# A row softmax in 64 tiles: sixteen narrow loads at the start, and a new order of the last two tiles

## The chip, the cores and the metric

The kernel runs on one core of a Trainium2 chip. The time is device time in microseconds (us) of one execution, and the median of several executions is what is compared. Besides the times there is a profile of one execution: it lists every instruction of each engine with its start and length, and every packet that the core's 16 DMA engines moved. The compute engines that matter here are VectorE (called DVE in the profile) and ScalarE (ACT). SyncE (SP) computes nothing; it issues the DMA transfers.

## The reference

The input is `logits`, 16 x 256 x 32,768 numbers in fp32, and a temperature, which is 1.0. The output is the softmax over the last axis:

```python
scaled = logits / temperature
scaled = scaled - scaled.max(axis=-1, keepdims=True)
exp_scaled = np.exp(scaled)
return (exp_scaled / exp_scaled.sum(axis=-1, keepdims=True)).astype(np.float32)
```

There are 4096 rows of 32,768 numbers, 512 MB in (536.87 million bytes) and as much out. Every number is read once and written once.

## The kernel before, in words

**Tiling.** Each row is cut into two halves of 16,384 numbers, which gives 8192 half rows; neighbours belong to one row. 128 half rows, one for each partition, make a tile of 8 MB. There are 64 tiles, numbered 0 to 63, and three buffers for them (`_BUFS`); tile g lives in buffer g mod 3, and everything is done in place: loaded, exponentiated, scaled and stored from the same memory.

**Work on a tile** (`compute`, lines 120 to 202). The tile is handled in K = 4 pieces of 4096 columns.
- For each piece VectorE takes the negated maximum of every partition (line 133) and ScalarE then computes exp(x - maximum of the piece) in place, with the sum of the piece beside it (line 146). Before its first maximum VectorE waits for the load.
- Then come the totals of the tile, a chain of small steps that passes between the engines: VectorE swaps the maxima and sums of neighbouring partitions, so that both halves of a row know all eight pieces (line 157), and takes the maximum over the eight (line 161); ScalarE computes the eight correction factors (line 168); VectorE sums factor times piece sum (line 174) and takes the reciprocal (line 186).
- At last VectorE multiplies every piece by its factor and by the reciprocal (line 193, "scaling" below).

**Order of the work.** It is written out by hand. Each engine runs its own instructions in program order and waits on semaphores. All transfers, loads and stores, are issued by SyncE into one queue, in the order of the list that `transfers` returns:

- L0 L1 L2, then S0 in two halves, L3 in two halves, S1, S2,
- then L4 S3, L5 S4, and so on up to L61 S60,
- then L62, L63, S61, S62, and S63 in four quarters.

A load of tile g (line 214) is issued once the store of tile g - 3 has landed, since they share a buffer. A store (line 223) is issued once all scaled pieces that it covers are done. Because the issuing engine goes through the list in order, a transfer that isn't ready holds up all that stand behind it. The transfers in the queue are carried out by 16 DMA engines at the same time, each of which takes a share of every transfer's rows in the queue's order.

**Where the change acts.** At the beginning L0 is one transfer of 128 rows x 16,384 columns, and `compute(0)` waits for all of it before its first maximum. At the end the engines' order is: everything of tile 62 (maxima, exponentials, totals, four scalings), then everything of tile 63. S62 needs four scaled pieces of tile 62; each quarter of S63 needs one scaled piece of tile 63.

Of the kernel before, what the change touches and what calls it, by code (L numbers as in the profile page):

```python
# [8 lines left out]
_W = 16384  # L9
_BUFS = 3  # L10
_PIECE = 4096
_LAST_STORE = 4096


class Stream:


    def __init__(self, nc, engine, name):
        self.engine = engine
        self.sem = nc.alloc_semaphore(name)  # L20
        self.count = 0
        self.seen = {}
# [38 lines left out]
def transfers(n):  # L61
    half = _W // 2  # L62
    whole = [(0, _W)]  # L63
    halves = [(0, half), (half, half)]
    quarters = [(s, _LAST_STORE) for s in range(0, _W, _LAST_STORE)]
    plan = [("L", 0, whole), ("L", 1, whole), ("L", 2, whole)]
    plan += [("S", 0, halves), ("L", 3, halves), ("S", 1, whole), ("S", 2, whole)]
    for i in range(4, n - 2):
        plan += [("L", i, whole), ("S", i - 1, whole)]
    plan += [("L", n - 2, whole), ("L", n - 1, whole)]  # L70
    plan += [("S", n - 3, whole), ("S", n - 2, whole), ("S", n - 1, quarters)]
    return plan


@with_exitstack
def kernel(
    ctx: ExitStack,
    tc: tile.TileContext,
    logits: bass.AP,
    temperature: bass.AP,  # L80
    out: bass.AP,
):
    nc = tc.nc
    inv_t = 1.0 / float(temperature)
    P = nc.NUM_PARTITIONS
    fp32 = mybir.dt.float32
    Exp = mybir.ActivationFunctionType.Exp
    A = mybir.AluOpType

    xf = logits.flatten_outer_dims()  # L90
    of = out.flatten_outer_dims()
    N, V = xf.shape
    assert V == 2 * _W and (N * 2) % P == 0
    x = xf.rearrange("n (h v) -> (n h) v", h=2)
    o = of.rearrange("n (h v) -> (n h) v", h=2)
    G = N * 2 // P
    K = _W // _PIECE
    swap = [i ^ 1 for i in range(32)]

    ctx.enter_context(tc.tile_critical())  # L100
    X = nc.alloc_sbuf_tensor("xs", [P, _BUFS * _W], fp32)
    T = [nc.alloc_sbuf_tensor(f"t{q}", [P, 4 * K], fp32) for q in range(2)]
    E = [nc.alloc_sbuf_tensor(f"ee{q}", [P, 2 * K], fp32) for q in range(2)]
    J = [nc.alloc_sbuf_tensor(f"junk{q}", [P, 2 * K], fp32) for q in range(2)]
    R = [nc.alloc_sbuf_tensor(f"row{q}", [P, 4], fp32) for q in range(2)]

    sp = Stream(nc, nc.sync, "sp")
    dve = Stream(nc, nc.vector, "dve")
    act = Stream(nc, nc.scalar, "act")
    loads = Lanes(nc, "ld")  # L110
    stores = Lanes(nc, "st")
    landed = {}
    stored = {}
    scaled = {}
    hist = {}

    def overlapping(parts, s, n):
        return [token for (a, m), token in parts.items() if a < s + n and s < a + m]

    def compute(g):  # L120
        base = (g % _BUFS) * _W
        t, e, j_, r = T[g % 2], E[g % 2], J[g % 2], R[g % 2]
        tv = t[:, 0 : 4 * K].rearrange("p (a b k) -> p a b k", a=2, b=2)
        old = hist.get(g - 2)
        if old:
            dve.wait(*old)
        sums = None
        for k in range(K):
            s = k * _PIECE
            xs = X[:, base + s : base + s + _PIECE]  # L130
            dve.wait(*overlapping(landed[g], s, _PIECE))
            m = dve.done(
                nc.vector.tensor_reduce(  # L133
                    out=t[:, k : k + 1], in_=xs, axis=mybir.AxisListType.X, op=A.max, negate=True
                )
            )
            if inv_t != 1.0:
                dve.wait(m)
                m = dve.done(
                    nc.vector.tensor_scalar_mul(  # L140
                        out=t[:, k : k + 1], in0=t[:, k : k + 1], scalar1=inv_t
                    )
                )
            act.wait(m)
            sums = act.done(
                nc.scalar.activation(  # L146
                    out=xs,
                    in_=xs,
                    func=Exp,
                    bias=t[:, k : k + 1],  # L150
                    scale=inv_t,
                    accum_out=t[:, K + k : K + k + 1],
                )
            )
        dve.wait(sums)
        sh = dve.done(
            nc.vector.stream_shuffle(out=t[:, 2 * K : 4 * K], in_=t[:, 0 : 2 * K], mask=swap)  # L157
        )
        dve.wait(sh)
        mx = dve.done(  # L160
            nc.vector.tensor_reduce(  # L161
                out=r[:, 0:1], in_=tv[:, :, 0, :], axis=mybir.AxisListType.XY, op=A.min
            )
        )
        act.wait(mx)
        ev = e[:, 0 : 2 * K].rearrange("p (a k) -> p a k", a=2)
        ee = act.done(
            nc.scalar.activation(  # L168
                out=ev, in_=tv[:, :, 0, :], func=Exp, bias=r[:, 0:1], scale=-1.0
            )  # L170
        )
        dve.wait(ee)
        tr = dve.done(
            nc.vector.tensor_tensor_reduce(  # L174
                out=j_[:, 0 : 2 * K].rearrange("p (a k) -> p a k", a=2),
                in0=ev,
                in1=tv[:, :, 1, :],
                scale=1.0,
                scalar=0.0,
                op0=A.mult,  # L180
                op1=A.add,
                accum_out=r[:, 1:2],
            )
        )
        dve.wait(tr)
        rc = dve.done(nc.vector.reciprocal(out=r[:, 2:3], in_=r[:, 1:2]))  # L186
        dve.wait(rc)
        scaled[g] = {}
        for k in range(K):
            s = k * _PIECE  # L190
            xs = X[:, base + s : base + s + _PIECE]
            scaled[g][s, _PIECE] = dve.done(
                nc.vector.tensor_scalar(  # L193
                    out=xs,
                    in0=xs,
                    scalar1=e[:, k : k + 1],
                    scalar2=r[:, 2:3],
                    op0=A.mult,
                    op1=A.mult,
                )  # L200
            )
        hist[g] = (ee, tr)

    for what, g, parts in transfers(G):
        base = (g % _BUFS) * _W
        rows = slice(g * P, (g + 1) * P)
        if what == "L":
            landed[g] = {}
            for k, (s, n) in enumerate(parts):
                if g >= _BUFS:  # L210
                    sp.wait(*overlapping(stored[g - _BUFS], s, n))
                landed[g][s, n] = loads.add(
                    (g % _BUFS, k),
                    nc.sync.dma_start(out=X[:, base + s : base + s + n], in_=x[rows, s : s + n]),
                )
            compute(g)
        else:
            stored[g] = {}
            for k, (s, n) in enumerate(parts):
                sp.wait(*overlapping(scaled[g], s, n))  # L220
                stored[g][s, n] = stores.add(
                    (g % _BUFS, k),
                    nc.sync.dma_start(out=o[rows, s : s + n], in_=X[:, base + s : base + s + n]),  # L223
                )
    sp.wait(*stores.tokens())
# [35 lines left out]
```

## Time and profile before

| what | value |
|---|---|
| median of 3 executions | 2514.72 us (2513.66 to 2514.77) |
| the profiled execution: its own time | 2513.76 us |
| its span, first to last instruction | 2512.0 us |
| moved by DMA | 1073.86 MB, 427 GB/s over the span |
| VectorE busy | 1755.7 us (70%) |
| ScalarE busy | 993.5 us (40%) |
| one maximum of a piece (line 133) | 4.41 us |
| one exponential of a piece (line 146) | 3.71 us |
| one scaling of a piece (line 193) | 2.41 us |

The profile's page gives busy times, the DMA traffic and groups of equal instructions. The other views are cut from the same execution: the *timeline* (instructions in order of time, with what ended the idle time before each), *windows* (busy time of each engine, share of time that the 16 DMA engines were busy, and GB/s, for a stretch of time), and the *DMA view* (packets of a stretch, and for the transfers issued in it the time from issue to landing; where there are several, the median). A DMA packet is counted in the stretch in which it starts, so a share over a short stretch can be above 1. A DMA transfer has landed when the last of its shares is through. A line such as `DVE t L133` means VectorE's work of line 133 that writes `t`. One core computes alone, and no other core's traffic is in the records.

### The profile page before, as it was taken

The numbers are of one execution on the slowest core, as the hardware profiler recorded it, in microseconds if no ns is written. First come the engines' busy times: TensorE is split into PE (matmuls) and PEld (weight loads), VectorE is DVE, ScalarE is ACT, GpSimd is POOL, SyncE is SP. The second block draws the span as 40 slices with busy tenths as digits, with TensorE's granted clock in tenths as the row PEclk, the third lists the DMA queues.
The fourth block names the chain that finished last, engine by engine and source line by source line (L and its number), as shares of the span: only waits on it lengthen the run. The fifth ranks groups of instructions, "written<-read, shape, count | busy, mean of one in ns | idle before, by whom it ended". The sixth has DMA issues, their size and how long they took to land.

```text
span 2512.0 us, 1661 instructions
## 1 busy us (share of the span) xinstructions
DVE 1755.7 (70%) x896; ACT 993.5 (40%) x577; POOL 0.2 (0%) x4
## 2 busy tenths in 40 slices
DVE  5866676766767667677676766777767676676776
ACT  3443342433424334243342433424334244342443
POOL 0000000000000000000000000000000000000000
DMA  9999999999999999999999999999999999999999
GB/s 409 443 427 432 434 432 432 425 432 432 420 433 425 429 431 422 432 424 430 433 421 431 434 427 425 434 431 422 433 432 421 431 422 433 433 420 432 434 420 389
DMA packets 19165, 1073.86 MB, mean 427 GB/s; under 512 B 2128, under 2 KB 2128, under 8 KB 2128
## 3 DMA queue, kind: packets, MB, share of 16 engines
q1 hardware_dynamic: 19152, 1073.75, 99.8%
q14 instruction: 13, 0.11, 0.0%
HBM read 536.87 MB, written 536.87 MB: 427 GB/s over the span
## 4 chain that ended last, share of the span: by engine, by line
DMA 57%; DVE 36%; ACT 5%; SPq 0%; issue 0%
DMA xs<-in_logits_dram 56%; DVE t L133 23%; DVE xs L193 12%; ACT xs L146 5%; DMA out_dram<-xs 1%; ACT ee L168 0%; SPq L223 0%; DVE row L186 0%; DVE row L161 0%; DVE t L157 0%; DVE junk L174 0%; DVE row L174 0%; SPq L256 0%; SPq L100 0%
## 5 line engine op out<-in xcount | busy, mean ns | idle before, releaser
L146 ACT ACTIVATE xs<-xs,t 128x4096 f32<-128x4096 f32 x256 | 949.2, 3708 | 1464.4 <-DVE t L133 1464.4
L133 DVE TENSOR_REDUCE t<-xs 128x1 f32<-128x4096 f32 x256 | 1113.4, 4412 | 462.1 <-DMA xs<-in_logits_dram 462.1
L193 DVE TENSOR_SCALAR xs<-xs,ee,row 128x4096 f32<-128x4096 f32 x256 | 600.4, 2409 | 2.3
L157 DVE LOAD_MASK_SELECT t<-t x64 | 0.9, 14 | 248.1 <-ACT xs L146 248.1
L146 ACT ACTIVATION_READ_ACCUMULATOR xs<-xs,t 128x1 f32 x256 | 47.7, 186 | 0.0
L168 ACT ACTIVATE ee<-t,row 128x8 f32<-128x8 f32 x64 | 19.2, 301 | 27.6 <-DVE row L161 27.6
L174 DVE CUSTOM_DVE_ANT_1 junk<-ee,t 128x8 f32<-128x8 f32 x64 | 10.7, 167 | 23.6 <-ACT ee L168 23.6
L186 DVE RECIPROCAL row<-row 128x1 f32<-128x1 f32 x64 | 10.5, 164 | 2.2
L161 DVE TENSOR_REDUCE row<-t 128x1 f32<-128x8 f32 x64 | 10.3, 161 | 2.2
L157 DVE STREAM_SHUFFLE t<-t 128x8 f32<-128x8 f32 x64 | 10.2, 160 | 0.0
L174 DVE DVE_READ_ACCUMULATOR2_ANT row<- 128x1 f32 x64 | 5.3, 83 | 0.0
L146 ACT ACT_TABLE_LOAD x1 | 1.3, 1283 | 0.9 <-SPq L100 0.9
L242 POOL MEMSET const-bfloat16-1.0<- 128x1 bf16 x1 | 0.1, 101 | 0.0
L242 POOL MEMSET const-uint8-127<- 128x1 uint8 x1 | 0.1, 101 | 0.0
L242 POOL MEMSET const-float32-0.0<- 128x1 f32 x1 | 0.1, 98 | 0.2 <-issue 0.2
L242 POOL MEMSET const-float32-1.0<- 128x1 f32 x1 | 0.1, 98 | 0.0
## 6 DMA issues: line engine op xcount, KB each, us to landing
out_dram<-xs SPq DMA_DIRECT2D x2, 4096.0 KB, 25.1
xs<-in_logits_dram SPq DMA_DIRECT2D x2, 4096.0 KB, 19.3
out_dram<-xs SPq DMA_DIRECT2D x4, 2048.0 KB, 10.8
xs<-in_logits_dram SPq DMA_DIRECT2D x63, 46.1
out_dram<-xs SPq DMA_DIRECT2D x62, 26.7
```

What stands on the lines that cost most here:

```text
L133: nc.vector.tensor_reduce(out=t[:, k : k + 1], in_=xs, axis=mybir.AxisListType.X, op=A.max, negate=True)
L146: nc.scalar.activation(out=xs, in_=xs, func=Exp, bias=t[:, k : k + 1], scale=inv_t, accum_out=t[:, K + k : K + k + 1],)
L157: nc.vector.stream_shuffle(out=t[:, 2 * K : 4 * K], in_=t[:, 0 : 2 * K], mask=swap)
L161: nc.vector.tensor_reduce(out=r[:, 0:1], in_=tv[:, :, 0, :], axis=mybir.AxisListType.XY, op=A.min)
L168: nc.scalar.activation(out=ev, in_=tv[:, :, 0, :], func=Exp, bias=r[:, 0:1], scale=-1.0)
L174: nc.vector.tensor_tensor_reduce(out=j_[:, 0 : 2 * K].rearrange("p (a k) -> p a k", a=2), in0=ev, in1=tv[:, :, 1, :], scale=1.0, scalar=0. ...
L186: rc = dve.done(nc.vector.reciprocal(out=r[:, 2:3], in_=r[:, 1:2]))
L193: nc.vector.tensor_scalar(out=xs, in0=xs, scalar1=e[:, k : k + 1], scalar2=r[:, 2:3], op0=A.mult, op1=A.mult,)
L242: nc = _bacc.Bacc("TRN2", target_bir_lowering=False, num_devices=1)
```

## The change

**At the start.** L0 covers the first 14,336 columns only. The last 2048 columns of tile 0 become an item of their own in the list ("N"), issued right behind: 16 transfers of 8 partitions each, in every group of 32 partitions the partitions j, j + 4, ..., j + 28 for j = 0 to 3. All 16 count on one semaphore. Tile 0's compute is written behind them; its pieces 0 to 2 now wait for the wide part alone, and piece 3 (columns 12,288 to 16,383) for both.

**At the end.** `compute` becomes a class `Tile` whose methods do what the sections of the old function did, in the same way: `exponentials` (maxima and exponentials of the pieces named), `totals`, and `scale`. Tiles 0 to 61 run them in the old order. For the last two tiles the order is

- exponentials of tile 62, all four pieces,
- exponentials of tile 63, the first piece,
- totals of tile 62,
- scaling of tile 62's pieces 0 and 1 on VectorE, and of its pieces 2 and 3 on ScalarE (`scale_on_act`: VectorE multiplies factor and reciprocal into one number for each partition, ScalarE multiplies the piece by it),
- exponentials of tile 63, the last three pieces, its totals, and its four scalings on VectorE.

SyncE's list keeps its order, and S62 now waits for both engines.

```diff
-    plan = [("L", 0, whole), ("L", 1, whole), ("L", 2, whole)]
+    wide = [(0, _W - _NARROW)]
+    plan = [("L", 0, wide), ("N", 0, [(_W - _NARROW, _NARROW)]), ("L", 1, whole), ("L", 2, whole)]
...
+        def scale_on_act(self, ks):
+            for k in ks:
+                xs = self.piece(k)
+                w = dve.done(
+                    nc.vector.tensor_tensor(
+                        out=self.j[:, k : k + 1], in0=self.e[:, k : k + 1], in1=self.r[:, 2:3], op=A.mult
+                    )
+                )
+                act.wait(w)
+                scaled[self.g][k * _PIECE, _PIECE] = act.done(
+                    nc.scalar.mul(out=xs, in_=xs, mul=self.j[:, k : k + 1])
+                )
+
+    every = list(range(K))
+
     def compute(g):
...
+        a = Tile(g)
+        if g == G - 2:
+            a.exponentials(every)
+            return a
+        if g == G - 1:
+            last = a
+            a = tiles[g - 1]
+            last.exponentials(every[:1])
+            a.totals()
+            a.scale(every[:2])
+            a.scale_on_act(every[2:])
+            last.exponentials(every[1:])
+            last.totals()
+            last.scale(every)
+            return last
+        a.exponentials(every)
+        a.totals()
+        a.scale(every)
+        return a
...
+            if what_next != "N":
+                tiles[g] = compute(g)
+        elif what == "N":
+            s, n = parts[0]
+            for q in range(0, P, 32):
+                for j in range(4):
+                    some = slice(q + j, q + 32, 4)
+                    landed[g][s, n] = loads.add(
+                        ("n",),
+                        nc.sync.dma_start(
+                            out=X[some, base + s : base + s + n],
+                            in_=x[g * P + q + j : g * P + q + 32 : 4, s : s + n],
+                        ),
+                    )
+            tiles[g] = compute(g)
```

More of the change, by code (lines that the diff above doesn't have):

```diff
@@ L12 @@
 _LAST_STORE = 4096
+_NARROW = 2048
 class Stream:
@@ L118, in overlapping, with __init__, piece, exponentials @@
         return [token for (a, m), token in parts.items() if a < s + n and s < a + m]
[L120 to L132, printed above, removed]
+    class Tile:
+        def __init__(self, g):
+            self.g = g
+            self.base = (g % _BUFS) * _W
+            self.t, self.e, self.j, self.r = T[g % 2], E[g % 2], J[g % 2], R[g % 2]
+            self.tv = self.t[:, 0 : 4 * K].rearrange("p (a b k) -> p a b k", a=2, b=2)
+            self.sums = None
+            scaled[g] = {}
+        def piece(self, k):
+            s = self.base + k * _PIECE
+            return X[:, s : s + _PIECE]
+        def exponentials(self, ks):
+            t = self.t
+            for k in ks:
+                if k == 0 and self.g >= 2:
+                    dve.wait(*hist[self.g - 2])
+                xs = self.piece(k)
+                dve.wait(*overlapping(landed[self.g], k * _PIECE, _PIECE))
+                m = dve.done(
+                    nc.vector.tensor_reduce(
+                        out=t[:, k : k + 1], in_=xs, axis=mybir.AxisListType.X, op=A.max, negate=True
+                    )
+                )
+                if inv_t != 1.0:
+                    dve.wait(m)
+                    m = dve.done(
+                        nc.vector.tensor_scalar_mul(
+                            out=t[:, k : k + 1], in0=t[:, k : k + 1], scalar1=inv_t
+                        )
+                    )
+                act.wait(m)
+                self.sums = act.done(
+                    nc.scalar.activation(
+                        out=xs,
+                        in_=xs,
+                        func=Exp,
+                        bias=t[:, k : k + 1],
+                        scale=inv_t,
+                        accum_out=t[:, K + k : K + k + 1],
+                    )
+                )
+        def totals(self):
+            t, e, r, tv = self.t, self.e, self.r, self.tv
+            dve.wait(self.sums)
+            sh = dve.done(
+                nc.vector.stream_shuffle(out=t[:, 2 * K : 4 * K], in_=t[:, 0 : 2 * K], mask=swap)
+            )
+            dve.wait(sh)
+            mx = dve.done(
@@ L133, in compute @@
                 nc.vector.tensor_reduce(
-                    out=t[:, k : k + 1], in_=xs, axis=mybir.AxisListType.X, op=A.max, negate=True
+                    out=r[:, 0:1], in_=tv[:, :, 0, :], axis=mybir.AxisListType.XY, op=A.min
                 )
             )
[L137 to L141, printed above, removed]
-                    )
-                )
@@ L144, in compute @@
[L144 to L152, printed above, removed]
-                )
[L154 to L199, printed above, removed]
-                )
-            )
@@ L202, in compute @@
-        hist[g] = (ee, tr)
-    for what, g, parts in transfers(G):
+            act.wait(mx)
+            ev = e[:, 0 : 2 * K].rearrange("p (a k) -> p a k", a=2)
+            ee = act.done(
+                nc.scalar.activation(
+                    out=ev, in_=tv[:, :, 0, :], func=Exp, bias=r[:, 0:1], scale=-1.0
+                )
+            )
+            dve.wait(ee)
+            tr = dve.done(
+                nc.vector.tensor_tensor_reduce(
+                    out=self.j[:, 0 : 2 * K].rearrange("p (a k) -> p a k", a=2),
+                    in0=ev,
+                    in1=tv[:, :, 1, :],
+                    scale=1.0,
+                    scalar=0.0,
+                    op0=A.mult,
+                    op1=A.add,
+                    accum_out=r[:, 1:2],
+                )
+            )
@@ new lines, in totals, with scale @@
+            dve.wait(tr)
+            rc = dve.done(nc.vector.reciprocal(out=r[:, 2:3], in_=r[:, 1:2]))
+            dve.wait(rc)
+            hist[self.g] = (ee, tr)
+        def scale(self, ks):
+            for k in ks:
+                xs = self.piece(k)
+                scaled[self.g][k * _PIECE, _PIECE] = dve.done(
+                    nc.vector.tensor_scalar(
+                        out=xs,
+                        in0=xs,
+                        scalar1=self.e[:, k : k + 1],
+                        scalar2=self.r[:, 2:3],
+                        op0=A.mult,
+                        op1=A.mult,
+                    )
+                )
@@ new lines, in scale_on_act @@
+        def scale_on_act(self, ks):
+            for k in ks:
+                xs = self.piece(k)
+                w = dve.done(
+                    nc.vector.tensor_tensor(
+                        out=self.j[:, k : k + 1], in0=self.e[:, k : k + 1], in1=self.r[:, 2:3], op=A.mult
+                    )
+                )
+                act.wait(w)
+                scaled[self.g][k * _PIECE, _PIECE] = act.done(
+                    nc.scalar.mul(out=xs, in_=xs, mul=self.j[:, k : k + 1])
+                )
@@ new lines, with compute @@
+    every = list(range(K))
+    def compute(g):
+        a = Tile(g)
[17 more added lines that the diff above has]
+        return a
@@ L205 @@
+    tiles = {}
+    plan = transfers(G)
+    for (what, g, parts), (what_next, _, _) in zip(plan, plan[1:] + [(None, None, None)]):
         base = (g % _BUFS) * _W
@@ L215 @@
                 )
-            compute(g)
+            if what_next != "N":
[11 more added lines that the diff above has]
+                        ),
+                    )
+            tiles[g] = compute(g)
         else:
```

## The prediction

> **What bounds the kernel now.** I read the page first (busy shares, DMA queue), then windows of the DMA traffic, then the landings of the last transfers, then the timeline of the tail. The page:
>
> ```profile
> DVE 1755.7 (70%) x896; ACT 993.5 (40%) x577; POOL 0.2 (0%) x4
> q1 hardware_dynamic: 19152, 1073.75, 99.8%
> ```
>
> VectorE and ScalarE have room; the one queue fills the sixteen DMA engines for 99.8% of the span. Of its 19,152 packets 2128 are under 512 B (133 transfers times 16 end marks). The other 17,024 are 125 x 128 whole rows, 4 x 128 half rows and 4 x 128 quarter rows: one packet is one row of one transfer, never split. A tile's 128 rows over 16 engines are 8 rows each. Two DMA views, of 5 to 57 us (loads only) and of 200 to 2400 us (loads and stores in turn):
>
> ```profile
> q1 hardware_dynamic: 383, 23.00, 102.1%
> q1 hardware_dynamic: 16191, 943.53, 100.1%
> ```
>
> 23.00 MB are 351 rows of 65,536 B; 1.021 x 52 us x 16 / 351 = 2.42 us a row. In the second, 14,397 rows give 2.447 us. An engine moves 2 x 64 x 8 = 1024 rows: 1024 x 2.42 = 2478 us of the 2512. The 0.027 us between the two rates, times 1024, is 28 us lost in the mixed stretch. So time goes down only if the slowest engine has less to move, loses less where loads and stores alternate, or waits less at the end.
>
> The tail: the DMA view at the issue of each of the last transfers (load of tile 63; stores of tile 61, of tile 62, and of the first and last quarter of tile 63; the number is us to landing), then SyncE's rows for the first, third and fourth, then a stretch:
>
> ```profile
> xs<-in_logits_dram SPq DMA_DIRECT2D x1, 39.3
> out_dram<-xs SPq DMA_DIRECT2D x1, 46.2
> out_dram<-xs SPq DMA_DIRECT2D x1, 26.8
> out_dram<-xs SPq DMA_DIRECT2D x1, 2048.0 KB, 6.9
> out_dram<-xs SPq DMA_DIRECT2D x1, 2048.0 KB, 14.5
> ...
> 2413.36 0.34 SPq L214 DMA_DIRECT2D xs<-in_logits_dram  x1
> 2464.52 0.34 SPq L223 DMA_DIRECT2D out_dram<-xs  x1
> 2489.25 0.33 SPq L223 DMA_DIRECT2D out_dram<-xs  x1
> ...
> 2486.00:2490.00 4.00, 3.56 (x6) 0.30 (x1) 0.00 (x0) 1.00 0.19 82
> ```
>
> Tile 63 lands at 2413.36 + 39.3 = 2452.7. Store 61 (issued 2425.82) lands at 2472.0, store 62 at 2491.3, the last quarter (issued 2496.22) at 2510.7: steps of 19.3 and 19.4, which are 8 rows of 2.42. So the slowest engine never pauses after 2452.7. But from 2486 to 2490 the share is 0.19: most engines had finished store 62 and waited for tile 63's first quarter, issued at 2489.25. The engines have drifted up to 5 us apart, and the late ones set the end.
>
> Tile 62's end on the compute engines (timeline):
>
> ```profile
> 2450.14 3.71 ACT L146 ACTIVATE xs<-xs,t 128x4096 f32<-128x4096 f32 x1 [0.53 <-DVE t L133]
> 2453.98 0.01 DVE L157 LOAD_MASK_SELECT t<-t  x1 [3.88 <-ACT xs L146]
> 2454.37 0.30 ACT L168 ACTIVATE ee<-t,row 128x8 f32<-128x8 f32 x1 [0.43 <-DVE row L161]
> 2455.11 9.38 DVE L193 TENSOR_SCALAR xs<-xs,ee,row 128x4096 f32<-128x4096 f32 x4
> 2464.41 4.41 DVE L133 TENSOR_REDUCE t<-xs 128x1 f32<-128x4096 f32 x1
> ```
>
> VectorE stands idle for 3.88 us, then needs 1.1 us for totals and 9.38 for scaling, and store 62 leaves at 2464.5, 7.5 us before store 61 lands: slack.
>
> **Part 1, the narrow transfers.** One transfer of 128 x 16,384 becomes one of 128 x 14,336 and 16 of 8 rows x 8 KB. The bytes stay. SyncE issues 16 more, 0.43 us each by its rows at the start (three in 1.33 us): 7 us, done by about 8.5 us, while the wide part keeps the engines busy until about 19. Loads 1 and 2 are queued behind, in time: nothing, but if the queue ran dry it would cost up to those 7 us. VectorE no longer waits for all of tile 0: its first three pieces need the wide part alone (7/8 of 19.3 us, so 2.4 earlier), the fourth comes 13 us later. That start is hidden anyway, since store 0 (issued 49.94) sits behind load 2 (landing 62.6): 0.
>
> What counts is who carries the narrow rows. A row is one packet, so a transfer of 8 rows occupies at most 8 engines. No such transfer is in the trace. Bounds: dealt in rotation, all engines get 8 x 8 KB each, 0 us. Always to the same eight, these move 16 x 8 KB = two rows' worth (4.84 us) in place of one (2.42), the other eight none: +2.4 us for eight engines, -2.4 for the rest. If the favoured eight held all the late engines, the slowest would come out up to 2.4 ahead: the lower end. I take +2.4, because all 133 transfers in the trace are dealt alike (16 marks each, the same form), with nothing that rotates; and engines that are 4.8 us behind at the start are then the ones that end the kernel. [...]
>
> **Part 2, the tail**, measured from T = landing of tile 63 (2452.7 before). Its order on VectorE is now: maximum of tile 63's first piece, totals of 62, two scalings of 62, two 128x1 products, three maxima of 63. On ScalarE the first exponential of 63 stands ahead of the small exponential of 62's totals, and two scalings of 62 ahead of the other three exponentials of 63.
> - The moved maximum would fill the 3.88 us of idle time, but cannot start at 2450.1: it waits for T, 2.6 us later. T + 4.4.
> - Exponential of that piece, 3.81 with its accumulator read: T + 8.3. Totals of 62 wait behind it on ScalarE; from there to the scaling 0.74 (2454.37 to 2455.11): T + 9.0.
> - Two scalings on VectorE, half of 9.38: T + 13.7. The first product 0.16 (as the reciprocal), 0.04 hand-over: T + 13.9.
> - Two scalings on ScalarE. Not in the trace; between VectorE's 2.41 and the exponential's 3.71. I take 3.71 (same engine, same size): T + 21.3. Store 62 waits for both engines: issued at 2474.0 instead of 2464.5, which is 2.0 after store 61 has landed.
> - From issue to landing on an idle queue: at least 8 rows, 19.4; at most 21.8 (the very first load). Taken 20.5: packets begin 0.8 after an issue (2489.25; none before 2490), then 19.4 and 0.3 for the mark. Store 62 lands at 2494.5 instead of 2491.3: **+3.2**. Bounds: +0.6 for ScalarE at VectorE's speed, +4.5 with the first load's price.
> - Tile 63 is late next, or not: ScalarE is free at T + 21.3, three exponentials 11.5, totals 1.2, one scaling 2.4: first quarter at T + 36.4 = 2489.1, before store 62 ends. It hides behind that store. The 2 us that VectorE gains on tile 63 are given back on ScalarE, and the pause of the early engines, which this edit would close, lies off the slowest engine: 0 gained.
>
> **Sum**: +2.4 + 3.2 = +5.6. Against the profiled execution (2513.76 in all, span 2512.0): 2519.4. That execution is 1.0 below the median of 2514.72, so on the median's scale 2520.3. The steady 2200 us I leave alone: 0, with -14 and +10 as the ends below.
>
> **Rivals.**
> - *Same: only the tail pays* (rows dealt evenly, or the relieved engines were the late ones): 2514.7 + 3.2 = 2517.9. For it: nothing shows which engines are late. Against: as above.
> - *Faster: eight engines behind by two rows lose less at the turns between loads and stores.* The pool is the 28 us. It decides from 10.6 recovered (5.6 + 5.0). Half of the pool: 2514.7 + 5.6 - 14 = 2506.3. For it: loads alone run at 2.42. Against: the share of 0.19 shows that the engines are already 5 us apart without it, and the 28 us are lost all the same.
> - *Slower still: the small transfers pay one by one.* If each of the 16 had to wait out the 0.8 us between issue and first packet, eight engines would be 13 us later: 2533. Or rows are read slower while the other half writes, +10: 2530. Against: successive loads in the queue land 19.4 apart with no pause between them. [...]
>
> **How the numbers follow.** The sum as worked out 0.55, own range 2517 to 2524 (tail +0.6 to +4.5, narrow part up to +5 with its marks); only the tail 0.17; faster 0.14; slower still 0.14. A difference of 0.2%, 5.0 us, is about what a measurement of this kernel can tell from no change; the forecast lies close to it, with 7 in 10 of its case beyond. Slower 0.385 + 0.14 = 0.53; same 0.165 + 0.17 = 0.33; faster 0.14. The range 2508 to 2530 leaves out about two thirds of the faster case and half of the slower still.
>
> **What would show it.** Store 62's issue about 21 us after tile 63's landing, ScalarE's two scalings near 3.7 us, an idle DMA stretch of 2 us or more before store 62's first packet, none before tile 63's. Tile 0's whole landing near 25.2 instead of 22.7. Tile 63's landing near 2455; at 2445 the turns have become cheaper, and the forecast is wrong by part 1; at 2453 the narrow rows were dealt evenly. Scalings of 2.4 us on ScalarE would take 2.6 from part 2.

## The result, and the profile after

The changed kernel takes 2520.8 us in the median of 8 executions (2518.5 to 2523.2). The kernel before, run 8 times beside it, takes 2513.7 (2512.2 to 2516.0). The ratio is 1.0027, interval 1.0016 to 1.0038: 6.8 us slower, 4.0 to 9.6. The forecast was 5.6 us slower.

The page of the kernel before has the first line, that of the changed kernel the others: the queue's packets, the sixteen transfers, and the new scalings on ScalarE.

```profile
DMA packets 19165, 1073.86 MB, mean 427 GB/s; under 512 B 2128, under 2 KB 2128, under 8 KB 2128
...
span 2519.4 us, 1680 instructions
DMA packets 19421, 1073.86 MB, mean 426 GB/s; under 512 B 2256, under 2 KB 2256, under 8 KB 2256
xs<-in_logits_dram SPq DMA_DIRECT2D x16, 64.0 KB
L228 ACT ACTIVATE xs<-xs,junk 128x4096 f32<-128x4096 f32 x2 | 7.3, 3700 | 5.3 <-DVE junk L222 5.3
```

There are 128 more end marks than the 2128 of before: 8 for each narrow transfer, where a wide one has 16. (An end mark is a packet of 4 bytes behind an engine's last row of a transfer; the kernel before has 133 x 16 = 2128.) So each narrow transfer went to eight engines.

The tail of the changed kernel: the DMA view at the issue of the load of tile 63, of store 61, of store 62, and of the first and last quarter of store 63 (us to landing); SyncE's rows for the first, third and fourth; and a window of the stretch before store 62.

```profile
xs<-in_logits_dram SPq DMA_DIRECT2D x1, 39.5
out_dram<-xs SPq DMA_DIRECT2D x1, 46.3
out_dram<-xs SPq DMA_DIRECT2D x1, 20.8
out_dram<-xs SPq DMA_DIRECT2D x1, 2048.0 KB, 11.1
out_dram<-xs SPq DMA_DIRECT2D x1, 2048.0 KB, 18.9
...
2417.05 0.34 SPq L266 DMA_DIRECT2D xs<-in_logits_dram  x1
2477.72 0.34 SPq L289 DMA_DIRECT2D out_dram<-xs  x1
2492.31 0.33 SPq L289 DMA_DIRECT2D out_dram<-xs  x1
...
2475.90:2478.50 2.60, 2.60 (x1) 2.60 (x2) 0.00 (x0) 1.00 0.00 0
```

Tile 63 lands at 2417.05 + 39.5 = 2456.6, which is 3.9 us later than before. Store 61 (issued 2429.53) lands at 2475.8. Store 62 is issued at 2477.7, 21.1 us after tile 63's landing, and in the 2.6 us before its first packets no data packet starts at all: the queue has run dry on every engine. Store 62 lands at 2498.5, and the last quarter, issued at 2499.28, at 2518.2. From tile 63's landing to the last landing it is 61.6 us; it was 58.1 before. So the profiled execution's 7.4 us of longer span are 3.9 ahead of that landing and 3.5 behind it; the 3.9 hold the scatter of two single executions too.

Why store 62 leaves so late is in the timeline of the changed kernel:

```profile
2456.59 4.42 DVE L144 TENSOR_REDUCE t<-xs 128x1 f32<-128x4096 f32 x1 [2.80 <-DMA xs<-in_logits_dram]
2461.05 3.71 ACT L157 ACTIVATE xs<-xs,t 128x4096 f32<-128x4096 f32 x1 [3.42 <-DVE t L144]
2464.76 0.28 ACT L182 ACTIVATE ee<-t,row 128x8 f32<-128x8 f32 x1
2465.48 4.73 DVE L208 TENSOR_SCALAR xs<-xs,ee,row 128x4096 f32<-128x4096 f32 x2
2470.32 7.31 ACT L228 ACTIVATE xs<-xs,junk 128x4096 f32<-128x4096 f32 x2 [5.28 <-DVE junk L222]
```

The first maximum of tile 63 waits 2.80 us for its data, tile 62's small exponential stands behind tile 63's large one, and the last two scalings of tile 62 are done one after the other on ScalarE until 2477.6.

At the start, the loads of tiles 1 and 2 (SyncE's rows, and us to landing). The first fence is the kernel before: the median of the three first loads, which is that of load 1, then load 2 alone. The second is the changed kernel: the sixteen narrow transfers, then load 1 alone.

```profile
xs<-in_logits_dram SPq DMA_DIRECT2D x3, 40.7
...
1.85 0.42 SPq L214 DMA_DIRECT2D xs<-in_logits_dram  x1
xs<-in_logits_dram SPq DMA_DIRECT2D x1, 60.8
```

```profile
1.37 10.79 SPq L277 DMA_DIRECT2D xs<-in_logits_dram  x16
12.21 0.44 SPq L266 DMA_DIRECT2D xs<-in_logits_dram  x1
xs<-in_logits_dram SPq DMA_DIRECT2D x1, 35.2
```

Load 1 lands at 12.21 + 35.2 = 47.4. Before, it was issued at 1.4 and landed at 42.1. That is 5.3 us of delay, not the 2.4 that the bytes account for. Of its sixteen end marks in the trace eight stand at 41.9 to 42.4 us and eight at 47.0 to 47.4: the narrow rows were indeed carried by the same eight engines. Load 2 then takes 19.3 us more (66.7), where it took 20.5 before (62.6).

### The profile page after: what moved, and what is told of

The parts are those of the page before. It is cut to its first block, busy times and chain, and to the rows that moved or that the text cites. A ratio compares the mean times of both kernels' runs of the same rounds, so it can differ in the third digit from the quotient of the medians.

```text
span 2519.4 us, 1680 instructions
## 1 busy us (share of the span) xinstructions
DVE 1751.1 (70%) x896; ACT 1000.4 (40%) x579; POOL 0.2 (0%) x4
## 4 chain that ended last, share of the span: by engine, by line
DMA 59%; DVE 34%; ACT 6%; SPq 0%; issue 0%
DMA xs<-in_logits_dram 55%; DVE t L144 21%; DVE xs L208 12%; ACT xs L157 5%; DMA out_dram<-xs 4%; ACT ee L182 0%; SPq L289 0%; ACT xs L228 0%; DVE row L200 0%; DVE row L175 0%; DVE junk L188 0%; DVE t L171 0%; DVE row L188 0%; SPq L266 0%; DVE junk L222 0%
## 5 line engine op out<-in xcount | busy, mean ns | idle before, releaser
L228 ACT ACTIVATE xs<-xs,junk 128x4096 f32<-128x4096 f32 x2 | 7.3, 3700 | 5.3 <-DVE junk L222 5.3
```

The source lines that it names most:

```text
L228: nc.scalar.mul(out=xs, in_=xs, mul=self.j[:, k : k + 1])
```

## The experiments

Executions of one kernel scatter by some 3 us to either side, nearly all of it gathered in the middle of the run: the landing of tile 63 lies anywhere from 2449.0 to 2452.7 in the four profiles here with the old start. So the price of a part is read in two ways: as a ratio over several executions, and from single profiles only as distances that lie close together in time (load 1, or tile 63's landing to the end). The edits are shown against the changed kernel where nothing else is said.

### The new tail alone

```diff
-    plan = [("L", 0, wide), ("N", 0, [(_W - _NARROW, _NARROW)]), ("L", 1, whole), ("L", 2, whole)]
+    plan = [("L", 0, whole), ("L", 1, whole), ("L", 2, whole)]
```

> Only the new order of the last two tiles; tile 0 is loaded by one transfer as before. Theory (store 62 leaves about 21.2 us after tile 63 has landed, when the queue has been empty for 2 us or more, and the narrow part is a separate price): tile 63 lands within about 1 us of the 2452.7 of before, store 62 is issued 21.2 us after it, the last store lands 65.4 to 65.8 us after it (58.1 before); the kernel is 3.2 us slower than before, 2.3 to 4.5. Rival (the narrow part makes the engines so late that the tail stalls; alone, the new order closes the early engines' pause and costs nothing): within 1 us of before, or up to 2 us faster.

Measured: ratio 1.0007, interval 0.9998 to 1.0016: 1.8 us slower, from 0.5 faster to 4.0 slower. In the profile tile 63 lands at 2449.0 (not within 1 us of 2452.7, as expected: that is the scatter above), store 62 leaves 21.2 us after it and lands 20.8 after that, as in the changed kernel, and the last landing is 61.6 us after tile 63's. (The expectation's 65.4 to 65.8 was a slip: 58.1 + 3.2 is 61.3.) So the tail stalls by itself, with no help from late engines, and costs 3.5 us by its own distances. The ratio alone can't tell that from nothing; it excludes the rival's 2 us of gain.

### The early maximum alone

Tile 62's four scalings stay on VectorE; only the first maximum and exponential of tile 63 move up.

```diff
             last.exponentials(every[:1])
             a.totals()
-            a.scale(every[:2])
-            a.scale_on_act(every[2:])
+            a.scale(every)
             last.exponentials(every[1:])
```

> Tile 0 loaded as before; in the tail only the first maximum and exponential of tile 63 stand ahead of tile 62's totals, and VectorE does all four scalings of tile 62. Theory (each step of the tail is worth what its place in the engines' order says): scaling of tile 62 starts 9.0 us after tile 63's landing, store 62 is issued 18.4 after it, about 0.9 before store 61 lands, and lands near 38.9 (38.6 before); tile 63's first quarter is issued near 38.9 after it and waits for nothing but VectorE, which makes the slowest engine wait 1 to 1.5 us; last landing 59.5 us after tile 63's (58.1 before, 61.6 with the whole new order): 1 to 2 us slower. Rival (the new order costs because of the early maximum alone): 3 us or more slower.

Measured: ratio 1.0010, interval 1.0001 to 1.0018, 2.5 us slower, 0.3 to 4.5. The chain by its rows: scaling starts 8.9 us after tile 63's landing, store 62 is issued at 18.3 and lands at 39.1, the first quarter is issued at 38.7, and the last lands at 59.7. That is 1.7 us more than the 58.1 of before. All steps came where the order of the engines puts them. By these distances, this half of the tail is worth about half of its 3.5 us (the ratio alone would leave room for the rival's 3 us); the rest comes in once the scalings on ScalarE have to wait behind the early exponential.

### The scalings on ScalarE alone

```diff
         if g == G - 2:
             a.exponentials(every)
+            a.totals()
+            a.scale(every[:2])
+            a.scale_on_act(every[2:])
             return a
-        if g == G - 1:
...
-            return last
```

Tile 63 then runs in the old order, and tile 0 is loaded by one transfer.

> Tile 0 loaded as before; in the tail only the scalings of tile 62's pieces 2 and 3 go to ScalarE, and the first maximum of tile 63 stays behind them. Theory (the slowest engine has no pause in the tail, so the early engines' pause is worth nothing): scaling starts 2.4 us after tile 63 lands as before, store 62 is issued at 14.6 us after it (11.8 before), still ahead of store 61's landing at 19.3; tile 63's first quarter is issued near 32 us after it (36.5 before) and no engine waits for it; the time is within 1 us of before. Rival (the pause of 4 us on most engines counts): 2 to 4 us faster.

Measured: ratio 1.0000, interval 0.9992 to 1.0009. The DMA view of this kernel at the issue of the load of tile 63, of store 62 and of the first quarter of store 63, SyncE's row for store 62, and the window in which most engines stood still before:

```profile
xs<-in_logits_dram SPq DMA_DIRECT2D x1, 39.3
out_dram<-xs SPq DMA_DIRECT2D x1, 24.1
out_dram<-xs SPq DMA_DIRECT2D x1, 2048.0 KB, 10.7
...
2466.04 0.34 SPq L280 DMA_DIRECT2D out_dram<-xs  x1
...
2484.00:2490.00 6.00, 6.00 (x4) 0.00 (x0) 0.00 (x0) 1.00 0.74 314
```

Store 62 leaves 14.6 us after tile 63's landing, while store 61 is still moving, and the first quarter leaves 32.9 us after it, 3.7 earlier than before. The stretch in which the share had been 0.19 over 4 us, or 0.38 over 6 us at the same distance from tile 63's landing, now has 0.74; instead the early engines wait ahead of store 62, where no packet starts from 2465.7 to 2466.7. And the last landing comes 58.1 us after tile 63's, exactly as before. The pause of the early engines was 4 us of idle time on most engines and worth nothing, since the latest engine had none.

### The narrow transfers alone

The tail's branches (`g == G - 2` and `g == G - 1`) are taken out; the start is that of the changed kernel.

> Only the sixteen narrow transfers; the last two tiles in the old order. Theory (eight engines carry two rows' worth in place of one, and half of their narrow rows are written at half rate): load 1 lands 5.3 us later than before (near 47.4), tile 63 about 4 us later, and the kernel is 3 to 5 us slower than before; the tail after tile 63's landing is that of before, 58.1 us to the last landing. Rival (only the bytes count, and the rest of tile 63's delay in the changed kernel was the scatter of one execution): 2.4 us slower. Second rival (the early lag is given back in the first tens of tiles): under 1 us.

Measured: ratio 1.0011, interval 1.0002 to 1.0020: 2.8 us slower, 0.5 to 5.0. Load 1 lands at 47.1, 5.0 us late; the tail is that of before, 58.1 us. Of the 5.0 us, 1.2 are back by the landing of load 2 and 2.8 by that of load 4; tile 63 lands 2.9 late in this execution. Nothing at all is excluded, and the full 5.0 us lie at the very end of the interval; between the theory's 3 to 5 and the rival's 2.4 it can't choose, and it doesn't quite exclude the second rival's "under 1".

### The same, with partitions 64 to 127 first

```diff
-            for q in range(0, P, 32):
+            for q in (64, 96, 0, 32):
```

> As the kernel with the narrow transfers alone, but the transfers of partitions 64 to 127 are issued ahead of those of partitions 0 to 63. In the changed kernel the traffic was at full rate from 19.6 to 22.0 us and at about 3/4 of it or less from 22.0 to 26.8. Theory (the eight engines write partitions 64 to 127 over a path that the other eight engines, which have begun load 1, also write): the slow stretch now comes first, from 19.6 to about 24.4, and from about 24.6 to 27 the rate is full again; load 1 lands as late, near 47.4. Rival (the slow rows are those that come late: too many small transfers in the queue, or reads that collide): full rate from 19.6 to 22 and slow after it, as in the changed kernel.

Windows of the DMA traffic while eight engines move narrow rows and the other eight have begun load 1. The last two numbers are the share of time with a packet and GB/s; a packet counts where it starts, so single windows are rough. First the narrow transfers in the change's order, then with partitions 64 to 127 first:

```profile
19.60:22.00 2.40, 1.63 (x1) 0.00 (x0) 0.00 (x0) 1.00 1.01 427
22.00:24.40 2.40, 2.40 (x1) 0.00 (x0) 0.00 (x0) 1.00 1.49 355
24.40:26.80 2.40, 2.40 (x2) 1.97 (x1) 0.00 (x0) 1.00 1.17 358
26.80:29.20 2.40, 2.40 (x2) 1.88 (x3) 0.00 (x0) 1.00 0.42 164
```

```profile
19.60:22.00 2.40, 1.31 (x1) 0.00 (x0) 0.00 (x0) 1.00 1.53 352
22.00:24.40 2.40, 2.40 (x1) 0.00 (x0) 0.00 (x0) 1.00 0.72 181
24.40:26.80 2.40, 2.40 (x2) 1.65 (x1) 0.00 (x0) 1.00 0.82 314
26.80:29.20 2.40, 2.40 (x1) 2.15 (x2) 0.00 (x0) 1.00 1.07 461
```

The full rate moved from the first window to the last, and the slow stretch moved forward with the transfers of the upper partitions. The rate is full again a little later than expected: the window from 24.4 us, 314 GB/s, still holds part of the slow stretch. Load 1 lands at 47.1 in the first order and at 47.3 in the second. So it isn't the number of small transfers in the queue, nor their lateness. That both sides write over one path was my guess; the windows show which rows are slow, not why.

The single packets in the trace of the changed kernel show what is slow. The eight engines move their first eight narrow rows at 0.31 us each, while the other eight move a whole row each in 2.42. From 22.5 us on, with the rows of partitions 64 to 127, the narrow rows take longer (0.61 to 0.64 us from 22.9 us on), and the whole rows that the other eight engines move meanwhile take 4.1 to 4.7.

### Only the rows of partitions 0 to 63 in narrow transfers

```diff
+    plan = [("U", 0, [(_W - _NARROW, _NARROW)]), ("L", 0, wide), ("N", 0, [(_W - _NARROW, _NARROW)]), ...
...
+                nc.sync.dma_start(out=X[64:128, base + s : base + s + n], in_=x[64:128, s : s + n]),
...
-            for q in range(0, P, 32):
+            for q in (0, 32):
```

> As the kernel with the narrow transfers alone, but partitions 64 to 127 get their last 2048 columns in one transfer of 64 partitions, first in the queue, and only partitions 0 to 63 get theirs in eight narrow transfers. The eight engines then carry one narrow row too many each and none of it into partitions 64 to 127. Theory (half rate only where two engines write the same partitions' path): load 1 lands 2.5 us later than before, near 44.6 (47.1 with sixteen narrow transfers), and the windows from 19.6 us on have no stretch below 400 GB/s. Rival (narrow transfers beside whole rows run at half rate wherever they go): a slow stretch behind the wide part and load 1 near 47.

```profile
7.70 0.92 SPq L258 DMA_DIRECT2D xs<-in_logits_dram  x2
xs<-in_logits_dram SPq DMA_DIRECT2D x1, 36.9
```

Load 1 lands at 7.70 + 36.9 = 44.6, as the theory said, 2.5 us later than before. The windows that held the slow stretch now read 386, 427, 444 and 437 GB/s; the first is under the 400 that I had named, but so is 14.8 to 17.2 us (382), where only the wide part's shorter rows are moved, so that is how packets are counted. The rows of the eight narrow transfers take 0.31 us each here, all of them. The transfer of 64 partitions is the slow one: it puts the landing of the wide part back to 23.3 us (20.3 with a narrow transfer of 128 partitions behind it), 2.9 us for 4 rows of 8 KB on each of 16 engines, which are 1.2 at the rate of the wide rows; in the trace its rows take 0.55 us on average, and about 0.6 from 4.0 us on. So the 2.5 us have two parts: the eight engines carry twelve narrow rows in place of eight (four too many, not one as the expectation says), 1.2 us at 0.31, and the four that go into partitions 64 to 127 take nearly twice that time. So rows of 8 KB for partitions 64 to 127 took about 0.6 us in both forms, in the transfer of 64 partitions on sixteen engines as in the transfers of 8 rows on eight, and narrow rows for partitions 0 to 63 beside whole rows took 0.31. The theory's path that two engines share is not shown. Two more things stay open. The rows of these partitions are also the upper rows of the tile in memory, so no run parts the place written to from the place read. And no run lets all sixteen engines move rows for partitions 0 to 63 alone.

### One narrow transfer of 128 partitions

```diff
-            for q in range(0, P, 32):
-                for j in range(4):
...
+            landed[g][s, n] = loads.add(
+                ("n",),
+                nc.sync.dma_start(out=X[:, base + s : base + s + n], in_=x[rows, s : s + n]),
+            )
```

> The last 2048 columns of tile 0 in one transfer of 128 partitions in place of sixteen of 8; old order of the tail. Theory (what costs is that eight engines carry the narrow rows, not that the tile is split or that its first maxima start earlier): load 1 lands within 0.3 us of the 42.1 of before, the time within 1 us of before. Rival (the smaller transfer or the earlier start of the compute is what is felt later): load 1 1 us or more late, 2 to 3 us slower in the end.

The four windows of the slow stretch taken as one, 326 GB/s with the sixteen narrow transfers, are here:

```profile
19.60:29.20 9.60, 8.84 (x3) 3.86 (x3) 0.00 (x0) 1.00 1.01 435
```

Measured: load 1 lands at 42.1, as before; ratio 0.9994, interval 0.9985 to 1.0003. The split of the load and the earlier first maximum (tile 0's wide part lands at 20.3) cost nothing and bring nothing that can be told. What costs is that eight engines carry the narrow rows.

### Loads and stores in pairs

The forecast's faster rival drew on 28 us lost in the mixed stretch. Was that pool real? Here the kernel before gets another order of its queue and nothing else:

```diff
-    for i in range(4, n - 2):
-        plan += [("L", i, whole), ("S", i - 1, whole)]
-    plan += [("L", n - 2, whole), ("L", n - 1, whole)]
-    plan += [("S", n - 3, whole), ("S", n - 2, whole), ("S", n - 1, quarters)]
+    for i in range(4, n, 2):
+        plan += [("L", i, whole), ("L", i + 1, whole), ("S", i - 1, whole)]
+        if i + 2 < n:
+            plan += [("S", i, whole)]
+    plan += [("S", n - 2, whole), ("S", n - 1, quarters)]
```

> Not the change but the pool that the forecast's faster rival drew on: the kernel before with loads and stores in pairs (two loads, then two stores) from tile 4 on, so that the queue turns between reading and writing half as often; tail as before. Theory A (the 28 us between the row time of loads alone, 2.42 us, and of the mixed stretch, 2.447, are paid at the turns): about 13 us faster, 8 to 16, and a row time near 2.433 from 200 to 2400 us. Theory B (they are paid wherever some engines read while others write, or with every row, however often the queue turns): within 2 us of before. Theory C (three buffers are too few for pairs): slower, with an idle stretch in the DMA windows.

Measured: 2497.4 us in the median, ratio 0.9937, interval 0.9923 to 0.9951: 15.8 us faster, 12 to 19. The DMA view from 200 to 2400 us:

```profile
q1 hardware_dynamic: 16276, 948.31, 100.2%
```

14,470 rows in 1.002 x 2200 us on 16 engines are 2.438 us a row, against 2.447 before and 2.42 for loads alone. The profiled execution, 2502.8 us, is one of the slowest of the six; in its steady stretch a third of the gap is gone, not the half that theory A names. By the median, half as many turns save about half of the pool, 0.26 us for each of some 60 turns left out. Theories B and C are out as they were put. But with the engines some 5 us apart (5.2 at tile 63 in the kernel before) and 19.3 us to a tile, some read while others write only near the turns, so whether the price is paid at the turn itself or in the few us around it, no run tells. This version beats both kernels.

### Pairs with one half of the tail, and pairs with the whole change

> Pairs, tile 0 loaded as before, and in the tail only the two scalings on ScalarE, with tile 63's first maximum behind them. Theory (turns are what the pairs save, and the early engines' pause in the tail is worth nothing): 14 to 18 us faster than before, the same as the pairs alone within 2. Rival (the pause counts): 18 to 21 us faster.

Measured: ratio 0.9940, interval 0.9928 to 0.9953, 15 us faster, 12 to 18: the same as the pairs alone within the intervals, and the last landing comes 58.0 us after tile 63's. The pause in the tail is worth nothing that can be told here either.

> The whole change on top of the order with two loads, then two stores. Theory (the turns and the change's two prices are separate): 16 us faster from the pairs, 5 to 6 us of it given back: 9 to 12 us faster than before; last landing 61.6 us after tile 63's. Rival (with half the turns the late engines no longer recover, or the narrow part's lag no longer matters): under 7, or over 14 us faster.

Measured: ratio 0.9972, interval 0.9960 to 0.9984, 7 us faster. The change gives back some 9 us of the pairs' gain; with the two intervals, that is 4 to 13. The tail's 61.6 us from tile 63's landing to the end stand there again. The 7 us lie below the theory's 9 to 12, at the edge of the rival's range, and the interval, 4 to 10, does not part them.

### The change once more, beside these

> The changed kernel once more, beside two others, to compare with the sum of its parts. Theory (the parts add up: 1.8 and 2.8 us as measured alone, 3.5 and 2.1 to 2.9 by their traces): 4.5 to 6.5 us slower than before. Rival (together they cost more than apart, because engines that start late also stall in the tail): 7 to 10 us slower.

Measured: ratio 1.0031, interval 1.0019 to 1.0042: 7.8 us slower, 4.8 to 10.6: by its middle in the rival's range, above the theory's 4.5 to 6.5, and the interval covers both. Its profile has load 1 5.0 us late, tile 63 3.7 us late and a tail of 61.6 us, the same parts as apart. The tail is thus no dearer when the narrow transfers go ahead of it. Whether the delay that is left at tile 63 (2.9 with the narrow transfers alone, 3.7 and 3.9 with the whole change) differs by more than the scatter stays open. All three are taken from one execution of the kernel before, the one with the latest landing of tile 63 among the four with the old start, so the true delay may be larger.

## Why the prediction was right

The time, 2520.3 against 2520.8, came out of a sum of two terms. One was right by its steps, the other by a bounded guess of which two errors cancelled, and that is luck. As a change, 5.6 us stand against 6.8: beside the changed kernel the kernel before took 2513.7, 1.0 less than the 2514.7 that the forecast started from, so the two times lie closer together than the two changes.

- **The tail, +3.2: right, step by step.** Store 62's issue was worked out as 21.3 us after tile 63's landing and came at 21.1; scalings on ScalarE were taken at 3.71 and took 3.70; issue to landing on an empty queue was taken as 20.5 and was 20.8. The queue stood empty for 2.6 us. Tile 63's first quarter (forecast at 36.4, came at 35.7) waited behind store 62. By its distances the tail costs 3.5 us. It was readable because every wait in it is of a fixed order on an engine.
- **Closing the early engines' pause, 0: right**, and shown by itself: the scalings on ScalarE alone close the pause ahead of store 63 and give a ratio of 1.0000 (0.9992 to 1.0009).
- **The earlier start of tile 0, 0: right** by the single narrow transfer.
- **SyncE's sixteen issues, 0: right in effect, wrong in size.** They took 10.79 us, 0.67 each, not 0.43; load 1 was queued at 12.2 us, still well ahead of need.
- **The narrow rows, +2.4: the sum is about right, the step behind it is not.** The ratio less the tail's 3.5 us leaves 3.3 for the start, and alone it cost 2.8 (0.5 to 5.0). The same eight engines did carry all the narrow rows, as taken. But half of these rows went into partitions 64 to 127, and while they moved both sides ran at about half rate: 0.61 to 0.64 us in place of 0.31 for a narrow row, 4.1 to 4.7 in place of 2.42 for the whole rows of the other eight. Load 1 was 5.0 to 5.3 us late, not 2.4. I had worked out bytes for each engine and nothing for the place of the rows. By the single packets each of the eight engines spent 4.5 us in the mean on its last eight narrow rows, those for partitions 64 to 127, in place of 2.5, and 0.2 to 0.7 us more than 2.42 on the whole row behind them. An estimate from these: 2.4 for the bytes, 2.1 and 0.2 to 0.7 make 4.7 to 5.2 us. Why both sides slowed down is not shown: no view tells which partitions a packet goes to, nor what the other eight engines wrote to meanwhile.
- **The late engines end the kernel: half right.** The forecast took it that the eight engines that are behind at the start are those that end the kernel. By the end marks in the trace, eight are 5.0 us or more behind the first from load 1 to 203 us, four of them have caught up by 577 us, and at tile 63 four are late, by 3.8 to 5.8 us. In the kernel before the marks are 0.5 us apart at load 1 and 5.0 at 572 us, and at tile 63 four engines are late as well, by 3.6 to 5.2. (In the other profiles it is two to eight.)
- **The steady stretch, 0: wrong by about as much the other way.** Load 2 follows load 1 by 19.3 us in the changed kernel and by 20.5 in the one before; load 4 likewise follows the store ahead of it in the queue by 19.3 (164.1 less 144.8) and not 21.2 (20.5 to 21.5 in the three other profiles with the old start). At both, a load is followed by a store. The staggered engines lose less at these first turns, and 2.9 of the 5.3 us are back at load 4. This is the mechanism of the faster rival, at work for two turns. After that the engines of the kernel before drift apart too, as the end marks just named show and the share of 0.19 in its tail had suggested, and the gain goes no further.
- **The rivals.** The tail alone is not the whole price (narrow transfers alone: 1.0002 to 1.0020). The small transfers did not pay one by one: the eight of partitions 0 to 63 ran at full rate (0.31 us for a row of 8 KB, 423 GB/s from 19.6 to 22.0 us). The same rival's +10, for rows read more slowly while others write, was a guess that no run shows. The pool behind the faster rival was real, as the pairs show, but stagger opens it for the first turns only.

One of the signs named beforehand was of little use. The landing of tile 63, "near 2455", came at 2456.6, and single executions with an unchanged start had it anywhere from 2449 to 2453: too coarse for the 2 us that it was to tell apart. Another tells more. The views give no landing for the narrow transfers, but the last of their end marks stands at 28.2 us in the trace, not near 25.2: the 3 us that the forecast had not counted.

## What to carry to other kernels

In a kernel bound by DMA, ask of every idle stretch whether the latest engine has it too; here 4 us of pause on most engines were worth nothing, and 2.6 us on all of them were paid in full. Moving a maximum into an idle slot is worth only what its data allow: look at when its load lands, and at what stands behind its follow-up on the other engine. And before the ends of a stream are polished, compare its row time with that of loads alone: 0.027 us a row was 28 us, more than both ends together, and another order of the same transfers brought 16 of them.

## What the runs showed of the hardware that I had not expected

- Narrow rows for partitions 64 to 127 on only eight engines were slow (0.61 to 0.64 us against 0.31 for partitions 0 to 63), and so were the whole rows that the other eight moved meanwhile (4.1 to 4.7 us against 2.42): 326 GB/s over 19.6 to 29.2 us with the sixteen narrow transfers, 435 with one transfer of 128 partitions.
- A transfer of 8 rows took SyncE 0.67 us to issue (sixteen in 10.79), one of 128 rows 0.33 to 0.57 in these runs.
- Each turn of the queue between loading and storing that was left out saved about 0.26 us (15.8 us over some 60 turns), though the engines are busy by the records all the time (a share of 1.00 from 200 to 2400 us): the lost time is inside slower rows, not in gaps. In the kernel before, from 200 to 2400 us, the median row takes 2.42 us and some 5% take more than 2.6.
- In the kernel before the sixteen engines of the queue drifted apart from 0.5 us at load 1 to 5.0 at 572 us. The last ended the load of tile 63 behind the first by 4.6 to 5.9 us in all the profiles here, with or without the narrow transfers.
